# Position bias table in 128 partitions and a quarter of the query rows, and a later place for the RG-LRU constants and the modulation pieces

## The chip, the core and the metric

The kernel runs on one core of one Trainium2 chip. Its time is the device time of one execution in microseconds; lower is better. The times shown are the median of three runs. The trace comes from one profiled execution and counts from its first instruction.

## What is computed

A hybrid layer is followed by two modulated transformer layers, all for 256 tokens (and 256 context tokens) of 1024 features in float32. Only the hybrid layer bears on this change:

```
h    = rms_norm(x, norm_g[0]);  proj = h @ w_in      # split into the inputs of three mixers
y_a  = rglru_mixer(...)      # log_a = -8 * r * softplus(-lam): constants of lam, then a scan over tokens
y_b  = nsa_mixer(...)        # 16 heads; every score has + tbl[rel_bucket(t - s)][head]
y_c  = gla_mixer(...)        # gated linear attention in chunks of 32 tokens
x    = x + rms_norm((sum of gates * (y @ w_branch)) @ w_out, norm_g[1]);  x = x + rms_norm(swiglu(...))
```

The position bias of the second mixer depends on the distance between query and key alone: one row of 384 distances per head holds it. The two layers behind need modulation columns, `silu(c) @ ada_w + ada_b`, of which nothing depends on the hybrid layer.

## The kernel before, in words

**Dense products.** All weights come as tiles of 128 partitions x 1024 float32 (512 KB). `wload` (line 62) issues the load on SyncE's DMA queue (line 68), casts the tile to a high part `wh` on ScalarE (line 71), subtracts it to a low part `wl` on VectorE (line 72), and TensorE makes three products per block (lines 104, 105, 108; for the 512 column form lines 371 to 373). The pools `wraw`, `wh` and `wl` hold three tiles each, so SyncE can issue the load of a tile only when the low part of the tile three places ahead is done.

**Background work.** The modulation columns are made without TensorE. A piece (`Ada.chunk`, line 1052) loads 128 x 512 float32 (256 KB, `araw`, line 1056, three buffers) and runs two multiply-and-sum instructions on VectorE (line 1059, output `junk`). The first layer has 144 such pieces. `K.rate` says how many pieces are put into the program for each tile of weights that `wload` takes; `K.credit` carries the fraction. Here the rate is 0.35 through the whole hybrid layer, from a credit of -5.

**What sets the order.** The program text is not the order on the engines: the build places instructions on each engine's queue by what is ready, and text that stands earlier has the first claim. So a piece that stands late in the text still moves ahead into places that the build takes for free. Each engine then runs its own queue strictly in that order, and a waiting instruction holds all that stand behind it, SyncE's loads too.

**The bias table.** `nsa_bias` (line 340) makes T[head, distance] by one product of the 32 x 16 table `rel` with a one-hot matrix, adds the mask `neg` (line 351) and has 16 partitions with 384 numbers. It then writes each head's row 128 times to DRAM, one copy per query row of a tile, in four DMAs of 32 copies (line 354). `rel_bias` (line 523) reads two heads back as [128 queries, head, 256 distances] in one DMA whose row step is 383 instead of 384, which shifts each query row by one distance. It runs once for each of the 8 chunks of two heads.

**The order in the text** (`Block1.run`): norm, key and value chunks of the compressed branch, the RG-LRU constants (`lru_prep`, line 641), queries, `nsa_rows` (eight small DMAs `x<-kvc` that turn keys into rows), keys woven with `compress_units` and `gla_decay` (its running sums are the four scans of line 757), values, the queries of the gated attention, `nsa_bias`, its values (`gla_v_units`, 8 tiles) and keys (line 785), gates, `gla_steps` (first mask copy on line 827), and then a weave of RG-LRU, merge and branch products with the attention of the second mixer (line 576 adds the bias to the scores). Names: `lrut`, `lsp`, `lbh` are RG-LRU's constants, `gk`, `gq`, `gt`, `gb`, `gatt` belong to the gated attention, `x`, `kvc`, `blk` to the compressed branch, `cs` and `ccth` are the modulation's two input vectors.

Of the kernel before, what the change touches and what calls it, by code (L numbers as in the profile page):

```python
# [7 lines left out]
F32 = mybir.dt.float32  # L8
# [6 lines left out]
P = 128  # L15
# pieces of background work for each tile of weights, in the kernel's parts
RATE1, RATE2, RATE3, RATE4, RATE5 = 0.35, 0.8, 0.3, 1.1, 0.0
CALM, NG1, NG2, LEAD, TAIL, NPRE, WARM, D1, D2 = 16, 14, 24, 3, 5, 2, 13, 2, 3
# steps of small dependent work after each piece of dense products
# [5 lines left out]
class Core:  # L25
    def __init__(self, tc, ctx, D):
# [8 lines left out]
        # work to be traced along with the weight tiles, rate pieces for each  # L35
# [6 lines left out]
        # the tensor engine's clock rises while the first data come in  # L42
# [12 lines left out]
    def preload(self, *srcs, low=None):  # L55
        """the weight tiles that the next calls of wload want, ahead of other work; low: the engine for l"""
# [23 lines left out]
    def fill(self, n):  # L80
        """trace the next n pieces of background work"""
        for _ in range(min(n, len(self.filler))):
            self.filler.pop(0)()

    def calm(self, n):
        """no background work along with n weight tiles, while a chain counts"""
        self.credit -= n * self.rate
# [11 lines left out]
    def mm3(self, out, wts, acts, start=True, stop=True):  # L99
        """out (+)= sum_k w_k^T a_k; wts: [(h, l)] with [128, M], acts: [(h, l)] with [128, N]"""  # L100
# [9 lines left out]
    def rsqrt_small(self, x, n, scale, eps=1e-6):  # L110
        """1/sqrt(x*scale + eps) for x [128, n] (SBUF or PSUM); for more than a few columns by Newton's steps"""
# [22 lines left out]
    def gelu2_steps(self, out, x, tmp):  # L134
        """out = 2 * gelu(x) (tanh form) in two steps; x, tmp, out in SBUF"""
# [8 lines left out]
    def sq_acc(self, accs, src, m):  # L144
        """squares of chunk m of 8: summed in accs[0], the last one apart in accs[1]"""
# [8 lines left out]
    def accs(self):  # L154
        """two [128, 256] sums of squares for 256 tokens"""
        return [self.sp.tile([P, 256], F32, tag=f"acc{i}", name=self.nm(f"acc{i}")) for i in range(2)]

    def rstd(self, accs, n, d):
        """[128, n / 128]: 1/sqrt(sum_p sum(accs)[p, t] / d + eps), tokens on partitions"""
# [8 lines left out]
    def bcast_rows(self, r):  # L168
        """r [128, n] per token as [128, n * 128] PSUM, the same on every partition"""
# [10 lines left out]
    def norm_mod_into(self, zh, zl, X, rb, G, S, ms=range(8)):  # L180
        """chunks ms of z = X*rstd*G + S split into (h, l) [128, 8, 256]; G, S(m): columns (S None: no shift)"""
# [16 lines left out]
    def stagger(self, first, second, norm, ahead):  # L198
        """pieces of the two segments' last products; the norm that follows is begun for the first segment
# [1810 lines left out]
```

## Time and profile before

| what | before |
|---|---|
| device time, median of 3 runs | 2429.65 us (2429.4 to 2430.14) |
| span of the profiled execution (first to last instruction) | 2420.2 us |
| TensorE busy | 2358.1 us (97%) |
| VectorE busy | 1717.1 us (71%) |
| ScalarE busy | 1050.3 us (43%) |
| GpSimd busy | 184.6 us (8%) |
| read from and written to HBM | 389.38 MB and 8.13 MB |

The trace gives the span of the profiled execution and no other time of it; the median of the timed runs is 9.45 us longer than that span. The busy shares are means over stages with different limits. [...]

### The profile page before, as it was taken

How to read it: one execution, taken by the hardware profiler on the slowest of the kernel's cores; microseconds unless marked ns; L12 is line 12 of the kernel's file. 1: busy time of each engine (PE TensorE's matmuls, PEld its weight loads, DVE VectorE, ACT ScalarE, POOL GpSimd, SP SyncE). 2: the span in 40 equal slices, each digit the busy share in tenths (PEclk: the TensorE clock that was granted, in tenths of full speed). 3: DMA queues.
4: the chain of work that ended last, by engine and by line, in shares of the span. 5: the costliest groups of instructions: out<-in, count | busy, mean ns of one | idle time of the engine just before them, and what ended most of it. 6: DMA issues, size and time to landing. Idle time of an engine off the chain costs nothing.

```text
span 2420.2 us, 38663 instructions
## 1 busy us (share of the span) xinstructions
PE 2358.1 (97%) x14647; PEld 2070.7 (86%) x14647; DVE 1717.1 (71%) x3622; ACT 1050.3 (43%) x1879; POOL 184.6 (8%) x207
## 2 busy tenths in 40 slices
PE   9969999999999999999999999999999999998999
PEld 8858988899999998889768888888988888877999
DVE  7946798768899976438787865656865755856555
ACT  5522477456444532226764422223522223665443
POOL 1100021111000100012330000000100000101000
PEclk8989999999999999999999999999999999998999
DMA  7884533366788664465313644444653533533664
GB/s 238 252 196 154 172 110 123 109 197 191 255 264 251 203 214 137 131 191 162 124 60 127 213 157 135 152 135 147 209 165 123 165 126 114 181 109 106 191 183 157
DMA packets 159110, 401.10 MB, mean 166 GB/s; under 512 B 26763, under 2 KB 42427, under 8 KB 158923
## 3 DMA queue, kind: packets, MB, share of 16 engines
q1 hardware_dynamic: 158923, 398.62, 52.8%
q8 instruction: 115, 1.88, 0.3%
q14 instruction: 72, 0.59, 0.1%
HBM read 389.38 MB, written 8.13 MB: 164 GB/s over the span
## 4 chain that ended last, share of the span: by engine, by line
PE 83%; DVE 6%; issue 4%; DMA 3%; ACT 2%; POOL 1%; SPq 1%; DVEq 0%; ACTq 0%; POOLq 0%
PE ps_mm L104 23%; PE ps_mm L108 23%; PE ps_mm L105 23%; DVE wl L72 2%; PE ps_mm L1201 2%; PE ps_mm L1202 1%; PE ps_mm L1203 1%; PE ps_at L1318 1%; DMA wraw<-in_w_in_n 1%; DVE junk L1059 1%; PE ps_mm L574 1%; DMA araw<-in_ada_w 1%; PE ps_mm L1680 1%; ACT wh L71 1%; PE ps_mm L1450 1%
## 5 line engine op out<-in xcount | busy, mean ns | idle before, releaser
L71 ACT CAST wh<-wraw 128x1024 fp32r<-128x1024 f32 (+2 forms) x603 | 604.5, 1003 | 780.0 <-PE ps_mm L108 389.4
L72 DVE TENSOR_TENSOR wl<-wraw,wh 128x1024 fp32r<-128x1024 f32 (+2 forms) x601 | 706.9, 1177 | 317.3 <-ACT wh L71 309.4
L104 PE MATMUL ps_mm<-zh,wh 128*128 128x256 f32 (+1 forms) x2568 | 765.9, 323 | 5.4 <-ACT zh L190 2.8
L105 PE MATMUL ps_mm<-zh,wl 128*128 128x256 f32 (+1 forms) x2568 | 759.8, 321 | 2.3 <-DVE wl L72 2.3
L104 PEld LDWEIGHTS ps_mm<-zh,wh 128*128 128x128 f32 x2568 | 489.0, 191 | 61.7 <-issue 13.7
L105 PEld LDWEIGHTS ps_mm<-zh,wl 128*128 128x128 f32 x2568 | 489.3, 191 | 41.9 <-DVE wl L72 3.5
L108 PE MATMUL ps_mm<-zl,wh 128*128 128x256 f32 (+1 forms) x2568 | 455.7, 320 | 0.0
L108 PEld LDWEIGHTS ps_mm<-zl,wh 128*128 128x128 f32 x2568 | 380.5, 190 | 39.0 <-issue 1.3
L1059 DVE SCALAR_TENSOR_TENSOR junk<-araw,cs 128x512 f32<-128x512 f32 x576 | 391.1, 692 | 13.9 <-DMA araw<-in_ada_w 6.6
L104 PE MATMUL ps_mm<-hh,wh 128*128 128x256 f32 (+1 forms) x1021 | 313.6, 329 | 0.9 <-ACT wh L71 0.9
L105 PE MATMUL ps_mm<-hh,wl 128*128 128x256 f32 (+1 forms) x1021 | 311.5, 327 | 1.0 <-DVE wl L72 0.9
L104 PEld LDWEIGHTS ps_mm<-hh,wh 128*128 128x128 f32 x1021 | 192.8, 189 | 21.6 <-ACT wh L71 1.1
L105 PEld LDWEIGHTS ps_mm<-hh,wl 128*128 128x128 f32 x1021 | 193.0, 189 | 19.4 <-DVE wl L72 1.4
L108 PE MATMUL ps_mm<-hl,wh 128*128 128x256 f32 (+1 forms) x1021 | 194.0, 327 | 0.0
L263 ACT ACTIVATE silu<-ps_mm 128x256 f32<-128x256 f32 (+1 forms) x124 | 58.8, 474 | 302.5 <-PE ps_mm L108 290.3
L108 PEld LDWEIGHTS ps_mm<-hl,wh 128*128 128x128 f32 x1021 | 156.6, 189 | 18.5 <-DVE hl L266 0.4
L1148 DVE SCALAR_TENSOR_TENSOR X<-ps_mm,adac,X 128x256 f32<-128x256 f32 x128 | 61.7, 482 | 128.2 <-PE ps_mm L108 126.9
L264 DVE TENSOR_TENSOR silu<-silu,ps_mm 128x256 f32<-128x256 f32 (+1 forms) x124 | 65.8, 531 | 110.0 <-PE ps_mm L108 109.6
L116 POOL TENSOR_TENSOR rs_v<-rs_v,power 128x2 f32<-128x2 f32 (+1 forms) x17 | 24.1, 1420 | 1054.3 <-ACT wh L71 709.6
L1201 PE MATMUL ps_mm<-wh,zh 128*128 128x512 f32 (+1 forms) x224 | 87.0, 388 | 0.0
L1202 PE MATMUL ps_mm<-wh,zl 128*128 128x512 f32 (+1 forms) x224 | 85.4, 381 | 0.0
L1203 PE MATMUL ps_mm<-wl,zh 128*128 128x512 f32 (+1 forms) x224 | 85.3, 381 | 0.0
(378 smaller groups left out, 2619.1 us busy)
## 6 DMA issues: line engine op xcount, KB each, us to landing
wraw<-in_up SPq DMA_DIRECT2D x204, 512.0 KB, 3.6
araw<-in_ada_w SPq DMA_DIRECT2D x288, 256.0 KB, 3.4
wraw<-in_w_in_t SPq DMA_DIRECT2D x72, 512.0 KB, 3.7
wraw<-in_dn SPq DMA_DIRECT2D x79, 448.0 KB, 3.3
wraw<-in_f_up SPq DMA_DIRECT2D x44, 512.0 KB, 4.3
wraw<-in_dn SPq DMA_DIRECT2D x40, 512.0 KB, 3.8
wraw<-in_ev_in SPq DMA_DIRECT2D x26, 512.0 KB, 3.4
wraw<-in_w_br SPq DMA_DIRECT2D x24, 512.0 KB, 4.0
```

What stands on the lines that cost most here:

```text
L71: nc.scalar.copy(h[:, :cols], raw[:, :cols])
L72: (low or nc.vector).tensor_tensor(out=l[:, :cols], in0=raw[:, :cols], in1=h.bitcast(F32)[:, :cols], op=ALU.subtract)
L104: nc.tensor.matmul(out, wh, ah, start=start and k == 0, stop=False)
L105: nc.tensor.matmul(out, wl, ah, start=False, stop=False)
L108: nc.tensor.matmul(out, wh, al, start=False, stop=stop and k == n - 1)
L263: nc.scalar.activation(g, pair[0], AF.Silu)
L264: nc.vector.tensor_tensor(out=g, in0=g, in1=ps, op=ALU.mult)
L1059: nc.vector.scalar_tensor_tensor(out=junk, in0=raw, scalar=1.0, in1=self.cs[:, s, h * 512:(h + 1) * 512], op0=ALU.mult, op1=ALU.mult, accu ...
L1148: self.nc.vector.scalar_tensor_tensor(out=X[:, m, :], in0=ps, scalar=self.ada.c[l][:, j, m, s:s + 1], in1=X[:, m, :], op0=ALU.mult, op1=AL ...
L1201: nc.tensor.matmul(ps[i], z.zh[:, k, tk], wh[:, w], start=k == 0, stop=False)
L1202: nc.tensor.matmul(ps[i], z.zl[:, k, tk], wh[:, w], start=False, stop=False)
L1203: nc.tensor.matmul(ps[i], z.zh[:, k, tk], wl[:, w], start=False, stop=k == 7)
```

## The change

The bias product gets its table widened on GpSimd: every head stands on 8 partitions, so that 128 partitions hold 16 heads x 8 equal rows. One DMA writes each of them 4 times: 32 rows per head in place of 128, 768 KB in place of 3072 KB. The read back is done per 32 query rows, four DMAs for each chunk in place of one. `lru_prep` moves behind the keys of the gated attention in the text. The modulation pieces have rate 0 up to the values of the gated attention, 1.2 from there, 0 in the weave with the second mixer's attention, and 1.2 again in the last eight tiles; the credit starts at 0. The mask constant has 128 rows instead of 16. The comments are gone from the new file, so its line numbers differ by a few.

```diff
-RATE1, RATE2, RATE3, RATE4, RATE5 = 0.35, 0.8, 0.3, 1.1, 0.0
+RATE1, RATE_GLA, RATE2, RATE3, RATE4, RATE5 = 0.0, 1.2, 0.8, 0.3, 1.1, 0.0
...
-            neg = self.a4("neg", shape=(16, 384))
+            neg = self.a4("neg", shape=(P, 384))
             nc.sync.dma_start(neg, K.D["relneg"])
-            ps = K.psum("at")
-            nc.tensor.matmul(ps[:16, :384], rel, oh, start=True, stop=True)
-            nc.vector.tensor_tensor(out=neg, in0=neg, in1=ps[:16, :384], op=ALU.add)
-            self.rscr = self.tc.dram_tile([16, 128, 384], F32, name="rel_scratch")
-            for q in range(4):
-                nc.sync.dma_start(self.rscr[:, q * 32:(q + 1) * 32, :], neg[:, None, :].to_broadcast([16, 32, 384]))
+            wide = self.s1("t1", (P, 260))[:32, :P].rearrange("p (h c) -> p h c", c=8)
+            nc.gpsimd.tensor_copy(wide, rel[:, :, None].to_broadcast([32, 16, 8]))
+            ps = K.psum("at")[:, :384]
+            nc.tensor.matmul(ps, wide.rearrange("p h c -> p (h c)"), oh, start=True, stop=True)
+            nc.vector.tensor_tensor(out=neg, in0=neg, in1=ps, op=ALU.add)
+            self.rscr = self.tc.dram_tile([P, 4, 384], F32, name="rel_scratch")
+            nc.sync.dma_start(self.rscr[:, :, :], neg[:, None, :].to_broadcast([P, 4, 384]))
...
-            self.nc.sync.dma_start(B, bass.AP(tensor=base.tensor, offset=base.offset + (8 * a + r) * 128 * 384 + 127,
-                                              ap=[[383, 128], [4 * 128 * 384, 2], [1, 256]]))
+            for p in range(0, P, 32):
+                self.nc.sync.dma_start(B[p:p + 32], bass.AP(
+                    tensor=base.tensor, offset=base.offset + (8 * a + r) * 32 * 384 + 127 - p,
+                    ap=[[383, 32], [4 * 32 * 384, 2], [1, 256]]))
...
         self.small_proj()
-        self.lru_prep()
...
         self.gla_rest()
+        K.rate = RATE_GLA
         for f in self.gla_v_units(0) + self.gla_v_units(1) + units(self.gla_k, 4):
             f()
         og = units(self.gla_o, 8)
+        self.lru_prep()
...
+        K.rate = 0.0
         seq = b2[4:] + l0 + [then(l1[0], *a0)] + l1[1:] + [then(mg[0][0], *a1)] + mg[0][1:6]
...
+        K.rate = RATE_GLA
         for m in range(8):
             self.branch(1, lambda: self.pairs(self.ny), m, True)
...
-            K.filler, K.rate, K.credit = [ada.prep] + ada.pieces(0), RATE1, -5.0
+            K.filler, K.rate, K.credit = [ada.prep] + ada.pieces(0), RATE1, 0.0
```

Three places show how the queues move. First SyncE's queue where the bias table is written, before the change:

```order
L68 DMA wraw_1390<-in_w_in_n 128x1024
L1056 DMA araw_3417<-in_ada_w 128x512
L1056 DMA araw_3650<-in_ada_w 128x512
L68 DMA wraw_1412<-in_w_in_n 128x1024
L354 DMA rel_scratch<-neg_1313 16x32x384 x4
L68 DMA wraw_1436<-in_w_in_n 128x1024
L68 DMA wraw_1454<-in_w_in_n 128x1024
L68 DMA wraw_1472<-in_w_in_n 128x1024
L529 DMA relb_2688<-rel_scratch 128x2x256
L529 DMA relb_2690<-rel_scratch 128x2x256
L68 DMA wraw_1499<-in_w_in_t 128x1024
```

The same place on SyncE's queue after the change:

```order
L68 DMA wraw_1327<-in_w_in_n 128x1024
L68 DMA wraw_1355<-in_w_in_n 128x1024
L356 DMA rel_scratch<-neg_1225 512x1x384
L68 DMA wraw_1379<-in_w_in_n 128x1024
L68 DMA wraw_1409<-in_w_in_n 128x1024
L1063 DMA araw_2230<-in_ada_w 128x512
L68 DMA wraw_1433<-in_w_in_n 128x1024
L1063 DMA araw_2298<-in_ada_w 128x512
L68 DMA wraw_1460<-in_w_in_t 128x1024
L1063 DMA araw_2355<-in_ada_w 128x512
L68 DMA wraw_1499<-in_w_in_t 128x1024
```

One write stands in place of four, and three of the eight `w_in_n` loads of the gated attention's values stand behind it, as they did before; the read backs have gone further down and modulation loads stand between the weights.

Second, SyncE's queue near the start, at the eight loads that turn keys into rows, before the change:

```order
L68 DMA wraw_400<-in_w_in_t 128x1024
L1040 DMA ng_103<-in_ng 128x48
L393 DMA x_55_470<-kvc_211 64x2x256
L68 DMA wraw_432<-in_w_in_t 128x1024
L394 DMA x_55_470<-kvc_211 64x2x255
...
L68 DMA wraw_480<-in_w_in_t 128x1024
L393 DMA x_56_475<-kvc_211 64x2x256
L394 DMA x_56_475<-kvc_211 64x2x255
...
L68 DMA wraw_512<-in_w_in_t 128x1024
```

And after the change:

```order
L68 DMA wraw_362<-in_w_in_t 128x1024
L1050 DMA cs<-in_cc 128x1024
L68 DMA wraw_394<-in_w_in_t 128x1024
L395 DMA x_55_432<-kvc_211 64x2x256
L396 DMA x_55_432<-kvc_211 64x2x255
...
L395 DMA x_56_437<-kvc_211 64x2x256
L396 DMA x_56_437<-kvc_211 64x2x255
...
L68 DMA wraw_442<-in_w_in_t 128x1024
L68 DMA wraw_474<-in_w_in_t 128x1024
```

The eighth weight tile (`wraw_480` before, `wraw_442` now) stood ahead of the second group of key rows (`x_56`) and now stands behind it, and the load of `cs` has come up to the sixth tile.

Third, VectorE's queue behind the sum of the bias table, before the change, with the low parts of the first tiles of the gated attention's values:

```order
L351 TENSOR_TENSOR neg_1313<-neg_1313,ps_at_1315 16x384
L776 TENSOR_TENSOR gt_740<-gb_741 128x1024
...
L72 TENSOR_TENSOR wl_1415<-wraw_1412,wh_1414 128x1024
L1069 TENSOR_TENSOR adac_106<-adac_106,ada_b 128x16
L72 TENSOR_TENSOR wl_1439<-wraw_1436,wh_1438 128x1024
L72 TENSOR_TENSOR wl_1457<-wraw_1454,wh_1456 128x1024
L72 TENSOR_TENSOR wl_1475<-wraw_1472,wh_1474 128x1024
L72 TENSOR_TENSOR wl_1502<-wraw_1499,wh_1501 128x1024
```

And after the change:

```order
L354 TENSOR_TENSOR neg_1225<-neg_1225,ps_at_1229 128x384
L780 TENSOR_TENSOR gt_702<-gb_703 128x1024
...
L72 TENSOR_TENSOR wl_1358<-wraw_1355,wh_1357 128x1024
L1066 SCALAR_TENSOR_TENSOR junk_2176,adapart<-araw_2174,cs 128x512
L1066 SCALAR_TENSOR_TENSOR junk_2178,adapart<-araw_2174,cs 128x512
L72 TENSOR_TENSOR wl_1382<-wraw_1379,wh_1381 128x1024
L1066 SCALAR_TENSOR_TENSOR junk_2232,adapart<-araw_2230,cs 128x512
L1066 SCALAR_TENSOR_TENSOR junk_2234,adapart<-araw_2230,cs 128x512
L1075 TENSOR_TENSOR adac_106<-adapart 128x16
L1076 TENSOR_TENSOR adac_106<-adac_106,ada_b 128x16
L72 TENSOR_TENSOR wl_1412<-wraw_1409,wh_1411 128x1024
```

Where the low parts of four tiles stood in a row, each now has two modulation instructions beside it. Counted over the whole queue from this sum to the first `gatt` copy, both orders hold 14 low parts; the modulation instructions are 19 before and 30 now. From the low part of the sixth tile to the scans of line 757 they are 20 before and 22 now, with 17 of the RG-LRU constants' instructions added, which stood ahead of the sixth tile. From the scans to the sum of the table the modulation instructions are 20 in both, with 11 of RG-LRU's added. At the 65th weight tile SyncE's queue has issued 51 modulation loads before and 54 now; at the 145th it is 53 and 54, and from the 155th on the two agree within two loads to the end.

## Rows read from the trace of the kernel before

**Rows 1.** The page's chain that ended last, by engine.

```profile
PE 83%; DVE 6%; issue 4%; DMA 3%; ACT 2%; POOL 1%; SPq 1%; DVEq 0%; ACTq 0%; POOLq 0%
```

**Rows 2.** Stretches: busy us (x instructions) per engine, clock, DMA share, GB/s.

```profile
28.57:76.84 48.27, 48.07 (x378) 45.65 (x378) 44.00 (x87) 31.64 (x46) 0.00 (x0) 1.00 0.89 289
76.84:116.15 39.31, 35.18 (x214) 30.36 (x213) 34.98 (x72) 19.22 (x25) 6.76 (x6) 0.91 0.77 244
129.96:153.07 23.11, 0.00 (x0) 0.00 (x0) 0.02 (x1) 1.04 (x1) 0.00 (x0) 0.61 0.93 151
153.07:185.02 31.95, 31.41 (x200) 28.11 (x200) 25.53 (x52) 14.40 (x18) 0.00 (x0) 0.91 0.82 265
288.20:476.80 188.60, 186.43 (x1346) 163.25 (x1346) 164.28 (x458) 119.95 (x303) 33.60 (x53) 1.00 0.37 118
```

**Rows 3.** TensorE in order of time: start, us, form, idle before and its end.

```profile
129.34 0.39 PE L372 MATMUL ps_mm<-wh,zl 128*128 128x512 f32 x1
129.57 0.39 PE L373 MATMUL ps_mm<-wl,zh 128*128 128x512 f32 x1
153.07 0.80 PE L371 MATMUL ps_mm<-wh,zh 128*128 128x512 f32 x1 [23.12 <-ACT wh L71]
...
158.75 0.40 PE L371 MATMUL ps_mm<-wh,zh 128*128 128x512 f32 x1
```

**Rows 4.** SyncE's queue in order of time, around the bias table's write.

```profile
116.72 13.21 SPq L354 DMA_DIRECT2D rel_scratch<-neg  x4
130.03 13.16 SPq L68 DMA_DIRECT2D wraw<-in_w_in_n  x3
150.53 0.89 SPq L529 DMA_DIRECT2D relb<-rel_scratch  x2
```

**Rows 5.** One stretch while the table is written, columns as in rows 2.

```profile
118.00:148.00 30.00, 11.96 (x53) 9.57 (x51) 5.86 (x12) 4.21 (x5) 0.00 (x0) 0.78 0.92 103
```

**Rows 6.** The table's DMAs: issue duration ns min/median/max, first and last start us.

```profile
L529 SPq DMA_DIRECT2D relb<-rel_scratch x8: 377/377/464, 150.5 to 429.9; - x8
L354 SPq DMA_DIRECT2D rel_scratch<-neg x4: 345/4040/4642, 116.7 to 125.6; - x4
```

**Rows 7.** DMA issues: count, KB each, median us from issue to landing.

```profile
wraw<-in_w_in_n SPq DMA_DIRECT2D x12, 512.0 KB, 3.5
...
rpb<-rpb_scratch SPq DMA_DIRECT2D x32, 64.0 KB, 3.1
```

**Rows 8.** VectorE in order of time, in the keys of the gated attention.

```profile
164.94 0.69 DVE L1059 SCALAR_TENSOR_TENSOR junk<-araw,cs 128x512 f32<-128x512 f32 x1
...
165.55 1.22 DVE L72 TENSOR_TENSOR wl<-wraw,wh 128x1024 fp32r<-128x1024 f32 x1
166.69 0.68 DVE L1059 SCALAR_TENSOR_TENSOR junk<-araw,cs 128x512 f32<-128x512 f32 x1
...
167.31 0.42 DVE L785 TENSOR_TENSOR gk<-ps_mm,gz 128x256 f32<-128x256 f32 x1
167.65 0.41 DVE L786 TENSOR_TENSOR gb<-ps_mm,gt 128x256 f32<-128x256 f32 x1
```

**Rows 9.** VectorE at the RG-LRU constants.

```profile
28.21 0.17 DVE L661 TENSOR_TENSOR lrut<-lrut 128x8 f32<-128x8 f32 x1
```

**Rows 10.** SyncE's queue, then ScalarE, at the eighth weight tile.

```profile
27.90 0.56 SPq L68 DMA_DIRECT2D wraw<-in_w_in_t  x1
30.08 0.60 SPq L393 DMA_DIRECT2D x<-kvc  x1
...
33.24 1.05 ACT L71 CAST wh<-wraw 128x1024 fp32r<-128x1024 f32 x1 [0.45 <-DMA wraw<-in_w_in_t]
...
41.51 0.38 ACT L418 ACTIVATE qT<-ps_mm 128x256 f32<-128x256 f32 x1 [0.55 <-PE ps_mm L108]
```

**Rows 11.** Windows in which the granted clock fell, columns as in rows 2.

```profile
80.00:90.00 10.00, 7.76 (x28) 6.39 (x29) 9.01 (x19) 5.32 (x8) 1.50 (x1) 0.68 0.58 183
...
200.00:210.00 10.00, 10.00 (x56) 9.25 (x55) 4.94 (x10) 2.29 (x4) 0.00 (x0) 0.68 0.25 80
```

More of the change, by code (lines that the diff above doesn't have):

```diff
@@ L1877, in _shape_constants @@
     C["onehot"] = oh
-    neg = np.zeros((16, 384), np.float32)
+    neg = np.zeros((128, 384), np.float32)
     neg[:, 256:] = -1e30
```

## The prediction

> **What bounds the kernel now.** I began with the chain of waits: 83% of it is TensorE [rows 1], so a change can gain only where TensorE stands still or runs at its lower clock. I then looked at the span in short stretches for such places in the hybrid layer, since from the 155th weight tile on the order of loads is the same within two. There is one large place: from 129.96 to 153.07 us TensorE does nothing, and neither do the other engines, while the DMA engines are 93% busy [rows 2]. TensorE's own rows show the end of it: the idle time of 23.12 us ended with a cast, which had waited for a weight tile [rows 3]. SyncE's queue shows why the tile was late: the four writes of the bias table occupy its issue for 13.21 us, the next three weight loads go out from 130.03 us on, and the read back, which waits for the last write, at 150.53 us [rows 4]. The first write was issued in 345 ns, the later ones took some 4 us each [rows 6], so the queue was full. The writes are what fills it: 4 x 786,432 B = 3.15 MB at 103 GB/s [rows 5] is 30.5 us, from 116.72 to about 147 us, with the DMA engines 92% busy all the time. Weights move at 289 GB/s at a share of 0.89 [rows 2].
>
> The stall has a tail. Before it, matmuls of 512 columns start 0.23 us apart. The 12 from 153.07 to 158.75 us take 5.68 us instead of 12 x 0.23 = 2.76 us [rows 3], 2.92 us more, and the mean clock of the idle stretch is 0.61 [rows 2]. The stall and its tail are 23.12 + 2.92 = 26.0 us.
>
> **The change part by part.**
>
> *The write.* It carries a quarter, 786,432 B. At the weights' 289 GB/s that is 2.7 us, at the rate of the old write, 103 GB/s, 7.6 us. What must hide it: when the table was ready, five of the eight tiles of values were loaded or loading, which kept TensorE at work from 116.7 to 129.96 us, 13.3 us. The sixth tile has to land and be split in that time: 3.5 us [rows 7] and then 1.05 us for the cast [rows 10] and 1.22 us for the low part [rows 8], 5.8 us. With the write ahead of it that is 8.5 to 13.4 us: hidden at the one end, 0.1 us late at the other. I take 0; without the cover it would cost its 2.7 to 7.6 us. Then the stall and its tail go: **-26.0 us**.
>
> Which end is nearer depends on why the old write was slow, and no row tells that apart from a slow DRAM side, as every long stretch at 103 GB/s is this one write from 16 partitions. [...]
>
> *The wide table* is one GpSimd copy (that engine is busy 8% of the span) ahead of a product that has the same 384 columns, and the larger mask is 168 KB more to load early, 0.6 us of DMA at 289 GB/s; the sum on VectorE has the same 384 elements per partition. Nothing of it is waited for longer: 0.
>
> *The read back* is four issues of 64 KB for one of 256 KB. One issue now holds SyncE 377 ns [rows 6], four 1.5 us, 1.1 us more for each of eight chunks. In the weave TensorE works 186.43 of 188.60 us [rows 2], with a weight tile each 2.9 us or more (24 products of 256 columns, each half of the 0.23 us of 512) on three buffers, and so 1.1 us more in the queue is hidden. I take 0, with 8 x 1.1 = 9 us as the price if no buffer covered it.
>
> *RG-LRU's constants and the modulation pieces, first stretch.* From the sixth tile's low part (28.57 us) to the scans (76.84 us) VectorE gets 2 more modulation instructions and 17 of RG-LRU's. Price from the rows: a modulation instruction takes a place of 0.61 us (164.94 to 165.55) [rows 8], one of RG-LRU's 0.17 us [rows 9]: 1.2 + 2.9 = 4.1 us. VectorE is busy 44.00 of 48.27 us there, so 4.3 us are free [rows 2]. All of it may fit, or all may be late, since the engine runs strictly in order; the DMA engines are at 0.89 here too. Bounds 0 to 4.1 us, nearer the low end as the free time is just enough: **+1.5**. From there to the sum (76.84 to 116.15 us) 11 of RG-LRU's at 0.17 us, 1.9 us, meet 4.3 us free: 0.
>
> *The eighth weight tile.* Its load went out at 27.90 us and now stands behind the second group of key rows, whose first goes out at 30.08 us as soon as ScalarE has the last chunk; four issues at 0.60 us put it to about 32.5 us, 4.6 us later [rows 10]. The cast at 33.24 us had waited for this tile [rows 10]. With 1.05 us for it and 1.22 us for the low part the tile was ready by about 35.5 us, and TensorE took it for the product that ends at 41.51 us, so from about 41.5 - 2.9 = 38.6 us. Of 4.6 us, 3.1 are covered: 0 to 1.5 us, I take the middle, **+0.8**.
>
> *Values and keys of the gated attention.* From the sum (116.15 us) to the first mask copy (185.02 us) VectorE gets 11 more modulation instructions, 30 for 19: 11 x 0.61 = 6.7 us. Its whole work there becomes 14 x 1.14 (low parts, 165.55 to 166.69) + 30 x 0.61 + 8 x 0.34 (key products, 167.31 to 167.65) [rows 8] + some 2.5 for the rest = 39.5 us. TensorE's time for the stretch, without the stall and its tail, is 68.9 - 26.0 = 42.9 us. It fits with 3.4 us to spare, by a margin of 8%. The DMA engines are as close: 14 tiles, 15 pieces, the write, two read backs and RG-LRU's weights are 13.1 MB, at 289 GB/s 45 us, at a share of 1 (289/0.89 = 325) 40 us. Bounds 0 to 6.7 us; nearer the low end, since it fits in both sums: **+2.0**. Behind it, up to the weave, the same 11 instructions are gone, where TensorE hardly waits: 0.
>
> *The later parts.* In the weave no modulation piece stood before and none stands now, so the rate 0 there changes nothing; behind it the loads agree within two. 0.
>
> **Sum.** -26.0 + 1.5 + 0.8 + 2.0 = -21.7 us. Against the profiled span that is 2420.2 - 21.7 = 2398.5 us; the runs are 9.45 us longer than this span, so the median comes to 2429.65 - 21.7 = **2408.0 us**.
>
> **The rivals.**
>
> *More is given back.* If VectorE's order costs all of its bounds, 4.1 + 1.5 + 6.7 = 12.3 us come back: 2429.65 - 26.0 + 12.3 = 2416.0 us, and with one more fall of the clock of the kind in rows 11 (68% over 10 us, so 3.2 us lost) 2419. For it: VectorE was busy 91% of the first stretch already. Against it: the counts fit.
>
> *More is gained.* Two windows at a clock of 0.68 [rows 11] cost 3.2 us each, and TensorE idles 4.1 us between the scans and the sum [rows 2]. Three low parts instead of two now stand ahead of the scans. If one fall and half of the idle time go and nothing else comes, the time is 2403.6 - 3.2 - 2.0 = 2398 us.
>
> *It does not do what it says.* If SyncE's issue stays blocked, because 512 rows of 1.5 KB occupy it as before whatever their source, or the table comes later than now, the stall is only moved: 2425 to 2430 us. Against it: the first of the four writes left SyncE after 345 ns [rows 6].
>
> *Slower.* The read back holds SyncE's queue in the weave. If the four parts landed one after another, each in the 3.1 us of a 64 KB read back of a similar table [rows 7], and SyncE could not go on before, 12.4 us per chunk would meet two tiles' cover of 5.8 us: 6.6 us for each of 7 chunks, 46 us, and 2408 + 46 = 2454 us. It decides from 26.5/7 = 3.8 us per chunk on. Against it: SyncE waits for buffers, not for landings, and one read back held it 377 ns.
>
> **How the numbers follow.** The forecast (2403 to 2412 us) has 0.65, more given back (2412 to 2420) 0.16, more gained (2396 to 2403) 0.11, not doing what it says 0.05, slower 0.03. From 2398 to 2418 us holds four fifths and reaches into both neighbours. Runs of this kernel tell 0.2%, 4.9 us, from no change: faster by more 0.92, within it 0.05 (most of the third rival), slower 0.03.
>
> **What the changed profile would show.** The write: one issue under 1 us, no stretch of 10 us without TensorE between 110 and 170 us, no long stretch of DMA at 100 GB/s. The given back: TensorE waits on a low part around 38 us, before the scans, and in the gated attention's keys, each under 4 us, with VectorE over 95% busy there. The weave as long as now, near 188 us. I am wrong if TensorE still waits over 8 us for a `w_in_n` tile, if the waits on low parts sum to over 10 us, or if the weave grows.

## The result and the profile after

| | before | after |
|---|---|---|
| median of the timed runs | 2429.89 us (2429.4 to 2431.06, 4 runs) | 2396.89 us (2394.53 to 2397.43, 4 runs) |
| ratio, 95% interval | | 0.9872 (0.9852 to 0.9892) |
| span of the profiled execution, clock | 2420.2 us, 0.985 | 2395.7 us, 0.990 |
| TensorE busy | 2358.1 us | 2356.5 us |
| written to HBM | 8.13 MB | 5.77 MB |

The kernel is faster by 33.0 us in the medians and by 24.5 us between the two profiled executions. The forecast was 21.7 us and 2408.0 us: the direction is right, the time is 11.1 us below the forecast and 1.1 us below the low end of its range.

The chain that ended last on the page after, by engine. TensorE's share has risen from 83% to 88%, and "issue" has fallen from 4% to 1% [rows 1]:

```profile
PE 88%; DVE 5%; DMA 2%; ACT 2%; POOL 2%; issue 1%; SPq 0%; ACTq 0%; DVEq 0%; POOLq 0%
```

Stretches of the kernel after, columns as in rows 2: around the write, the weave, and one window to which I come back.

```profile
110.00:170.00 60.00, 60.00 (x380) 53.33 (x380) 54.64 (x124) 24.20 (x29) 0.31 (x1) 0.98 0.87 281
262.93:451.50 188.57, 186.49 (x1346) 163.31 (x1345) 164.43 (x458) 119.89 (x303) 33.40 (x53) 1.00 0.39 118
40.00:50.00 10.00, 9.37 (x44) 8.26 (x45) 6.77 (x13) 5.54 (x11) 0.00 (x0) 0.66 0.69 225
```

TensorE is busy in all of the 60 us from 110 to 170, where it stood still for 23 us before, and the DMA engines move 281 GB/s there; while the old table was written they moved 103 GB/s [rows 5]. The weave has the length and the busy time that it had [rows 2]. SyncE's queue around the write of the kernel after: one issue of 0.58 us where four took 13.21 [rows 4], and the next weight loads go out 2.3 us after it.

```profile
118.16 2.02 SPq L68 DMA_DIRECT2D wraw<-in_w_in_n  x2
121.40 0.58 SPq L356 DMA_DIRECT2D rel_scratch<-neg  x1
123.67 2.69 SPq L68 DMA_DIRECT2D wraw<-in_w_in_n  x2
```

The read backs (the view of line 532: duration in ns, minimum, median, maximum) are 32 for 8 [rows 6]; under "who waited for it" that view names no engine.

```profile
L532 SPq DMA_DIRECT2D relb<-rel_scratch x32: 325/420/669, 141.4 to 406.3; - x32
```

To compare stages I use three marks on TensorE: the first product with `zh`, the table's product and the first transpose of `gb` in the gated attention. They are these rows of before,

```profile
115.30 0.81 PE L350 MATMUL ps_at<-oh,rel 32*16 32x384 f32 x2
178.63 0.60 PE L795 MATMUL ps_at<-ident,gb 128*128 128x128 f32 x4
```

and these of after:

```profile
13.79 0.58 PE L104 MATMUL ps_mm<-zh,wh 128*128 128x256 f32 x1 [1.01 <-ACT zh L190]
...
119.87 0.58 PE L353 MATMUL ps_at<-oh,t 32*128 32x384 f32 x1
...
157.03 0.60 PE L799 MATMUL ps_at<-ident,gb 128*128 128x128 f32 x4
```

From the table's product to `gb` it was 178.63 - 115.30 = 63.33 us and is 157.03 - 119.87 = 37.16 us: -26.2 us. From the first product (13.41 us before) to the table's product it was 101.89 us and is 106.08 us: +4.2 us. The first product itself starts 0.4 us later, and what is behind `gb` takes 2.9 us less: 26.2 - 4.2 - 0.4 + 2.9 = 24.5 us.

### The profile page after: what moved, and what is told of

The parts are those of the page before. It is cut to its first block, busy times and chain, and to the rows that moved or that the text cites. A ratio compares the mean times of both kernels' runs of the same rounds, so it can differ in the third digit from the quotient of the medians.

```text
span 2395.7 us, 38691 instructions
## 1 busy us (share of the span) xinstructions
PE 2356.5 (98%) x14647; PEld 2072.7 (87%) x14647; DVE 1715.2 (72%) x3622; ACT 1049.3 (44%) x1879; POOL 183.7 (8%) x208
## 3 DMA queue, kind: packets, MB, share of 16 engines
HBM read 389.56 MB, written 5.77 MB: 165 GB/s over the span
## 4 chain that ended last, share of the span: by engine, by line
PE 88%; DVE 5%; DMA 2%; ACT 2%; POOL 2%; issue 1%; SPq 0%; ACTq 0%; DVEq 0%; POOLq 0%
PE ps_mm L104 24%; PE ps_mm L105 24%; PE ps_mm L108 24%; PE ps_mm L1208 2%; PE ps_mm L1210 2%; PE ps_mm L1209 2%; DVE wl L72 1%; PE ps_at L1325 1%; PE ps_mm L1457 1%; PE ps_mm L578 1%; PE ps_at L1314 1%; ACT wh L71 1%; DMA wraw<-in_up 1%; DVE junk L1066 1%; PE ps_mm L1687 1%
## 5 line engine op out<-in xcount | busy, mean ns | idle before, releaser
L1066 DVE SCALAR_TENSOR_TENSOR junk<-araw,cs 128x512 f32<-128x512 f32 x576 | 391.0, 693 | 11.1 <-DMA araw<-in_ada_w 3.7
```

The costliest lines, as they stand in the source:

```text
L1066: nc.vector.scalar_tensor_tensor(out=junk, in0=raw, scalar=1.0, in1=self.cs[:, s, h * 512:(h + 1) * 512], op0=ALU.mult, op1=ALU.mult, accu ...
```

## The experiments

**Two parts of a run's time.** Every timed run has a span and a mean granted clock, as a share of TensorE's full clock. Span x clock is the time at full clock that the run's stretches are worth; span x (1 - clock), the rest, is what the lower clock took, and where TensorE stands still at the lower clock it counts a part of that idle time too. The clock is on record with three decimals, so both parts are uncertain by 1.2 us in a single run. The table has the mean of these two over the runs of each kernel, and its two stages (first product to table's product, table's product to `gb`) from its profiled execution, for the second row from the first profile of before. Device times are 1.7 to 1.9 us above the spans throughout.

| kernel | runs | median us | ratio (95%) | span x clock | rest | to the table | to `gb` |
|---|---|---|---|---|---|---|---|
| before, as its own run | 10 | 2426.34 | 1.0005 (0.9989 to 1.0021) | 2384.9 | 40.5 | 100.1 | 63.4 |
| before, beside the others | 46 | 2425.0 to 2428.9 | 1 | 2385.0 to 2385.4 | 38.5 to 41.9 | 101.9 | 63.3 |
| after, first | 4 | 2396.89 | 0.9872 (0.9852 to 0.9892) | 2370.7 | 23.9 | 106.1 | 37.2 |
| after, again | 5 | 2397.96 | 0.9874 (0.9849 to 0.9898) | 2369.8 | 27.3 | 103.1 | 37.2 |
| table alone | 4 | 2404.13 | 0.9912 (0.9887 to 0.9938) | 2370.4 | 31.2 | 100.1 | 37.2 |
| moves alone | 9 | 2429.4 | 1.0027 (1.0007 to 1.0046) | 2386.9 | 42.4 | 100.1 | 63.9 |
| table and constants | 6 | 2397.22 | 0.9878 (0.9857 to 0.99) | 2369.7 | 27.6 | 101.3 | 37.2 |
| table and rates | 4 | 2408.18 | 0.9914 (0.9888 to 0.994) | 2372.5 | 34.3 | 102.6 | 37.2 |
| eighth tile first | 10 | 2403.75 | 0.9933 (0.9905 to 0.9961) | 2369.6 | 37.1 | 101.3 | 37.2 |
| all rows, 128 partitions | 4 | 2407.96 | 0.9919 (0.9892 to 0.9946) | 2377.4 | 30.7 | 103.2 | 39.3 |
| quarter, 16 partitions | 6 | 2411.59 | 0.993 (0.9904 to 0.9956) | 2373.8 | 36.6 | 103.5 | 37.2 |
| after, 1.9 us later | 6 | 2409.84 | 0.9925 (0.9904 to 0.9945) | 2372.8 | 35.7 | 103.2 | 37.1 |
| after, 3.8 us later | 6 | 2413.67 | 0.9931 (0.9915 to 0.9947) | 2377.2 | 33.4 | 109.5 | 37.1 |

The delays of the last two rows are part of their column "to the table". The intervals of the table alone, table and rates, and all rows touch those of after, so that they differ from it is not beyond doubt; the intervals of the eighth tile first, the quarter and the two delays lie clear of it.

No kernel here leaves out any part of what has to be computed.

**The kernel before, once more.** No edit.

> The kernel before, unchanged, run once more as a run of its own, to see how its timed runs stand to its profiled execution. Its first profile had a span of 2420.2 us while its timed runs have a median of 2429.9 us; the changed kernel's runs are 1.7 us above their spans. If the timed runs of the kernel before have spans of about 2428 us, the 8 us lie inside the program and its profiled execution was a quick one; if their spans are about 2420 us and the times 2430 us, they lie around the program. The profile should show the idle time of TensorE of 23 us at about 130 us again.

Its ten runs have spans of 2420.4 to 2430.5 us and times of 2422.14 to 2432.34 us, 1.7 to 1.9 us above them. So the 8 us lie inside the program, and the profiled execution that I read was a quick one. Span x clock is 2383 to 2387 us in all ten; the rest, the time at the lower clock, goes from 34 to 46 us. In its profile TensorE stands still for 23.22 us at the write.

**The two halves of the change.** The table alone is after without the moves (first diff), the moves alone are after without the table's part (second):

```diff
-RATE1, RATE_GLA, RATE2, RATE3, RATE4, RATE5 = 0.0, 1.2, 0.8, 0.3, 1.1, 0.0
+RATE1, RATE2, RATE3, RATE4, RATE5 = 0.35, 0.8, 0.3, 1.1, 0.0
...
         self.small_proj()
+        self.lru_prep()
...
-            K.filler, K.rate, K.credit = [ada.prep] + ada.pieces(0), RATE1, 0.0
+            K.filler, K.rate, K.credit = [ada.prep] + ada.pieces(0), RATE1, -5.0
...
```

```diff
-            self.rscr = self.tc.dram_tile([P, 4, 384], F32, name="rel_scratch")
+            self.rscr = self.tc.dram_tile([16, 128, 384], F32, name="rel_scratch")
+            for q in range(4):
+                nc.sync.dma_start(self.rscr[:, q * 32:(q + 1) * 32, :], neg[:, None, :].to_broadcast([16, 32, 384]))
...
```

> The table's part of the change alone: 128 partitions, a quarter of the query rows, read back in four DMAs; RG-LRU's constants, the rates and the credit stay as before. Theory (the write's stall is the whole gain, and the moves cost some 4 to 6 us ahead of the sum and give some 4 us back behind it): the stall of 23.1 us and its tail of 2.9 us go, the table's product stands at 115.3 us as before, and the span is 2420.2 - 26.0 = 2394 us, within 3 us of the changed kernel's 2395.7; the eighth tile of values and keys costs no wait at 40 us. Rival 1 (the moves are part of the gain): without them the span stays above 2400 us, a ratio to before over 0.991. Rival 2 (the moves cost on balance): the span is 2390 us or less, faster than the changed kernel.

> The other part of the change alone: RG-LRU's constants, the modulation pieces' rates and the credit as in the changed kernel; the table is written for all 128 query rows from 16 partitions and read back in one DMA per chunk, as before. Theory: the stall at the write stays, 23 us of idle TensorE before a w_in_n tile, beginning some 5 us later than before because of the wait for the eighth tile near 40 us; the span is 2418 to 2426 us, ratio 0.998 to 1.002. Rival 1 (the moves are part of the gain): 2410 us or less, ratio below 0.996. Rival 2 (the moves cost): over 2424 us.

The moves alone keep the stall: TensorE's row of that kernel behind it is

```profile
153.62 0.80 PE L372 MATMUL ps_mm<-wh,zh 128*128 128x512 f32 x1 [23.62 <-ACT wh L71]
```

and its profiled span of 2422.8 us is that of the kernel before. The stall begins at 130.0 us as before, not 5 us later as I had expected, since no wait for the eighth tile came in this profile. Its ratio, 1.0027, lies just above what the theory allowed, and the mean span of its nine runs, 2429.3 us, is that of the rival by which the moves cost (over 2424 us); before has 2423.9 us beside it. Of the 5.4 us between them 1.5 are time at full clock and 3.9 the rest. The table alone has the same 37.16 us behind the table's product as the whole change, and a span x clock of 2370.4 us beside 2370.2 (the mean of the nine runs of after). So the table brings all of the gain at full clock, and the moves neither gain nor cost there by more than a microsecond or two. Its profiled span was 2396.1 us, as the theory had it (within 3 us of 2395.7). But its four runs spread from 2397.88 to 2407.58 us, with a mean span of 2401.6 us and a ratio of 0.9912, which is by the letter the rival that the moves are part of the gain. If they are, it is through the clock, and with these few runs that stays open.

**The missing combinations of the moves.** With the table's change go the rates alone (first diff against after: the constants are back) or RG-LRU's constants alone (second: rates and credit are back):

```diff
         self.small_proj()
+        self.lru_prep()
...
         og = units(self.gla_o, 8)
-        self.lru_prep()
```

```diff
-RATE1, RATE_GLA, RATE2, RATE3, RATE4, RATE5 = 0.0, 1.2, 0.8, 0.3, 1.1, 0.0
+RATE1, RATE2, RATE3, RATE4, RATE5 = 0.35, 0.8, 0.3, 1.1, 0.0
...
```

> The changed kernel with RG-LRU's constants back at their old place, so that the eighth tile is loaded between the two groups of key rows again; the table and the rates stay changed. If the wait for the eighth tile belongs to the moved constants, there is no wait near 40 us here, the table's product stands 100 to 102 us behind the first product, and the kernel is 3 to 6 us faster than the changed one of the same call. Rival (the constants' place does nothing that lasts): within 2 us of the changed kernel of the same call, apart from the spread of the granted clock.

> The table's change and RG-LRU's constants moved, with the modulation pieces' rates and credit as before: the piece that is missing between the table alone (2403 us at 0.987 on average, clock times span 2370) and the whole change (2398 us, 2370). Theory (the moved constants delay the eighth tile and nothing else, and the rest is the clock): TensorE waits near 40 us for 0.5 to 2 us, the first product to the table's product takes 102 to 106 us, clock times span is 2370 to 2374 us, and the median 2398 to 2410 us goes with the clock. Rival (the rates make the wait near 40 us): no wait there, 100 to 101 us to the table's product.

In neither does TensorE wait near 40 us. With the rates alone the table's product stands 102.6 us behind the first one, yet the kernel is not faster than after but 10 us slower in the median, at a rest of 34.3 us: the expectation that it would gain 3 to 6 us failed. With the constants alone the build leaves the eighth tile between the two groups of key rows, as before, so the theory for that run failed too: the late load comes only from both moves together, as the rates alone don't bring it either. Its rows on SyncE's queue:

```profile
26.92 0.55 SPq L68 DMA_DIRECT2D wraw<-in_w_in_t  x1
28.77 0.59 SPq L395 DMA_DIRECT2D x<-kvc  x1
```

**What made the old write slow: its source or its bytes.** Two kernels undo one of them each, all rows from 128 partitions and read back in one DMA per chunk (first), and a quarter of the rows from 16 partitions (second, where the product and the mask go back to 16 rows as well). Of each diff the write:

```diff
-            self.rscr = self.tc.dram_tile([P, 4, 384], F32, name="rel_scratch")
-            nc.sync.dma_start(self.rscr[:, :, :], neg[:, None, :].to_broadcast([P, 4, 384]))
+            self.rscr = self.tc.dram_tile([P, 16, 384], F32, name="rel_scratch")
+            nc.sync.dma_start(self.rscr[:, :, :], neg[:, None, :].to_broadcast([P, 16, 384]))
...
```

```diff
-            self.rscr = self.tc.dram_tile([P, 4, 384], F32, name="rel_scratch")
+            self.rscr = self.tc.dram_tile([16, 32, 384], F32, name="rel_scratch")
+            nc.sync.dma_start(self.rscr[:, :, :], neg[:, None, :].to_broadcast([16, 32, 384]))
...
```

> The changed kernel with the table written for all 128 query rows (16 copies from each of 128 partitions, 3.15 MB in one DMA) and read back in one DMA per chunk as before: only the source's partitions are changed, not the bytes. Theory 1 (the source of 16 partitions made the old write slow): it runs at 250 to 310 GB/s, takes 10 to 13 us, and TensorE stands still for 0 to 6 us at about 135 us; ratio to before 0.987 to 0.992. Theory 2 (the rows written in DRAM, 2,048 of 1.5 KB, make it slow): it runs at about 103 GB/s for 30 us, TensorE stands still for 20 to 24 us, and the time is that of the kernel before, ratio 0.997 to 1.002.

> The changed kernel with the quarter of the rows written from 16 partitions (32 copies of each, 786 KB in one DMA), read back in four DMAs: only the bytes are changed, not the source. Theory 1 (the source of 16 partitions is slow): it runs at about 103 GB/s for 7.6 us, and the weight tiles behind it land that much later; the cover of 13 us hides it but for 0 to 2 us of idle TensorE near 133 us, so the ratio to before is that of the changed kernel, or up to 0.001 above. Theory 2 (the bytes and rows make it slow): it runs as fast as the write from 128 partitions, at 250 GB/s or more, with no stretch of 5 us at about 100 GB/s. Either way the bytes alone would bring most of the 26 us.

With all rows from 128 partitions, the stretch behind the write's issue (columns as in rows 2), and TensorE's wait behind it:

```profile
122.46:131.00 8.54, 8.54 (x39) 7.07 (x38) 6.26 (x16) 2.89 (x4) 0.00 (x0) 1.00 1.03 367
```

```profile
134.91 0.50 PE L373 MATMUL ps_mm<-wh,zh 128*128 128x512 f32 x1 [1.47 <-ACT wh L71]
```

The DMA engines move 367 GB/s there, and TensorE loses 39.29 - 37.16 = 2.1 us in place of 26. The trace holds the write's 2,048 packets of 1,536 B: from the first to the end of the last they take 8.96 us, so 3.15 MB at 351 GB/s, where the same packets of the old write take 32.3 us. With a quarter of the rows from 16 partitions, one stretch, and VectorE's first low part behind it:

```profile
124.00:126.00 2.00, 2.00 (x10) 1.66 (x9) 1.85 (x5) 1.05 (x1) 0.00 (x0) 1.00 0.91 99
```

```profile
132.28 1.23 DVE L72 TENSOR_TENSOR wl<-wraw,wh 128x1024 fp32r<-128x1024 f32 x1 [3.49 <-ACT wh L71]
```

The rate is 99 GB/s, as slow as the old write's 103, at a DMA share of 0.91; the 512 packets take 7.6 us, and those of after 2.97 us. One packet takes 228 ns in the old write and 224 ns in this one, 65 ns in the two writes from 128 partitions (medians). So it is the source that makes the write slow, not the rows or the bytes. What changes along with its 16 partitions is how often one DMA repeats a source row: 32 times in both slow writes, 16 and 4 times in the fast ones. No run here separates the two. The stage to `gb` is 37.2 us all the same, so TensorE is covered. But VectorE stands idle for 3.5 us there. In the gated attention TensorE then waits 2.44 us for a mask copy, which stood behind a modulation instruction that had waited 1.31 us for its load. That this goes back to the slow write is not shown: with the table alone, too, TensorE waits 1.3 us for this copy.

So either half of the table's change takes nearly the whole stall away: the bytes alone 26.2 us of it, the source alone 24.1 us. The medians of the source alone and the bytes alone are 10 and 14 us above after; of that 7.2 and 3.6 us are time at full clock, the other part is the clock. Of the 7.2 us the stage to `gb` holds 2.1; where the others lie was not followed.

**The late eighth tile.** The load that RG-LRU's constants and the rates had pushed back is asked for first:

```diff
+        K.preload(K.D["w_in_t"][2])
         self.nsa_rows()
```

> The changed kernel with one load moved: the eighth of the first tiles of input weights is asked for ahead of the key rows' DMAs instead of behind them, which is where RG-LRU's constants had put it. Theory (the wait of 2.0 us near 40 us and the lower clock behind it, 0.66 in the window from 40 to 50 us, come from this late load): the wait is gone, the clock in that window is 0.9 or more, and the table's product stands 3 to 6 us earlier than the 119.9 us of the changed kernel; the span is 2391 to 2395 us. Rival (the lower clock or the wait comes from VectorE's order, with the modulation pieces and constants): TensorE waits as long at another place ahead of 60 us, and the span stays within 1.5 us of 2395.7 us.

> The changed kernel, unchanged, run and profiled once more beside the other runs of this call. In its first profile TensorE waited 2.0 us for the eighth tile at 40.6 us and ran at half clock behind it (6 us late at the table's product against the kernel before); with the moves alone (the profile of the run with the old table) the same order of loads cost no wait at all. Theory A (the wait is a close finish between the key rows' landing, VectorE's copies and the cast, and differs from one execution to the next): the wait at about 40 us is under 1 us here and the table's product stands 100 to 102 us behind the first product, for 106.1 in the first profile. Theory B (it belongs to the order): the wait is 1.5 to 2.5 us again and the product stands 104 to 107 us behind the first. Timed: a ratio of 0.985 to 0.992 to the kernel before.

These are rows of the first profile of after: SyncE, ScalarE and TensorE at the eighth tile.

```profile
33.01 1.72 SPq L68 DMA_DIRECT2D wraw<-in_w_in_t  x3
```

```profile
38.59 1.04 ACT L462 CAST blkh<-blk 128x1024 fp32r<-128x1024 f32 x1 [1.44 <-DVE blk L459]
39.54 1.04 ACT L71 CAST wh<-wraw 128x1024 fp32r<-128x1024 f32 x1
```

```profile
40.63 0.38 PE L104 MATMUL ps_mm<-zh,wh 128*128 128x256 f32 x1 [2.00 <-ACT wh L71]
```

The load goes out at 33.01 us, 5.1 us later than before [rows 10], but that is not what the tile waits for in the end. Its cast stands in ScalarE's queue behind the cast of `blkh`, which waits 1.44 us for VectorE's `blk`, and follows it without a wait of its own. VectorE had in turn waited for the key rows to land before its first copy of the group, 1.37 us in this profile, 0.67 us in the second one of after, and not at all in that of the shorter delay, where TensorE does not wait either. TensorE waits 2.00 us, and behind that the granted clock in 40 to 50 us is 0.66, 0.34 x 10 = 3.4 us lost. In the second profile of after the wait is

```profile
39.03 0.38 PE L104 MATMUL ps_mm<-zh,wh 128*128 128x256 f32 x1 [0.64 <-ACT wh L71]
```

and the clock there 0.83. The seven profiles with this order of loads have waits of 2.00, 0.64, 0.97, 1.57, 0, 1.85 and 0 us (after twice, all rows, quarter, the two delays, moves alone): a close finish, as theory A had it, which cost a wait in five of seven. The first stage is 100.1 us with the moves alone, where it does not come, and 106.1 and 103.1 us in after; the last lies between the two theories.

With the eighth tile first the wait for its cast is gone; TensorE waits 0.79 us for a low part at 44.26 us, and the clock in 40 to 50 us is 1.00. The table's product stands 101.3 us behind the first product, 4.8 and 1.8 us sooner than in the two profiles of after. Yet the median is 2403.75 us, 6 us above after, at the same span x clock (2369.6), with a rest of 37.1 us for 25.8. Neither the theory's span (2391 to 2395 us) nor the rival's is what was measured (2401.4).

**Small shifts.** The source of the last two kernels adds nothing but a delay: products of 128 columns ahead of the table's product, 8 or 16 of them (the diff has the first).

```diff
+            for _ in range(8):
+                nc.tensor.matmul(ps[:, :P], K.ones, K.ones, start=True, stop=True)
             nc.tensor.matmul(ps, wide.rearrange("p h c -> p (h c)"), oh, start=True, stop=True)
```

> The changed kernel with 8 more products of 128 columns on TensorE (their result is not used) just ahead of the table's product: 16 instructions at about 0.12 us each, a delay of 1.9 us, and nothing else changed. It asks why kernels whose time at full clock is alike (mean clock times span 2368 to 2376 us for all with a quarter of the rows) differ by 6 to 14 us in the median. Theory (small shifts decide which of the marginal falls of the granted clock come, in the gated attention and near 530, 780, 1230 and 1310 us): clock times span is 2372 us, 1.9 us above the changed kernel's 2370, but the median is 2403 to 2412 us, at a clock of 0.984 to 0.988. Rival (the falls belong to waits that the other versions have and this one doesn't): the median is 2398 to 2402 us at 0.988 to 0.990.

> The same with 16 more products, a delay of 3.8 us ahead of the table's product. Theory (small shifts decide): clock times span 2374 us, and the clock goes its own way again, 0.983 to 0.990, not in step with the delay of half the size. Rival (the falls belong to waits of the other versions): 2400 to 2404 us, 3.8 us above the changed kernel at the same clock.

The expectation had nothing else changed, but that is not so. The build, which places instructions by what is ready, gives the loads and VectorE's instructions another order in places. On SyncE's queue three weight loads stand in a row right ahead of the write with the shorter delay, two in after, and behind it two are left of the eight `w_in_n` loads, for three in after:

```profile
115.28 4.35 SPq L68 DMA_DIRECT2D wraw<-in_w_in_n  x3
```

With 1.9 us and that order the median is 12 us longer, with 3.8 us 16 us longer. Span x clock grows by 2.6 and 7.0 us, the rest by 10 and 8 us. The 7.0 us are more than the 3.8 expected; the wait of 1.85 us for the eighth tile is among them in its profile. The same 20 us of the gated attention, first in after, then with the delay of 1.9 us:

```profile
225.00:245.00 20.00, 19.94 (x158) 18.61 (x157) 13.93 (x24) 7.89 (x12) 1.64 (x1) 1.00 0.39 118
```

```profile
225.00:245.00 20.00, 20.00 (x87) 18.41 (x87) 5.17 (x11) 3.23 (x5) 1.65 (x1) 0.50 0.24 74
```

TensorE is busy the whole time in both, and with the delay also for all of the 35 us ahead; at a granted clock of 0.50, where after has 1.00, it gets through 87 products instead of 158. So the kernels with a quarter of the rows differ from each other by the clock, and a change as small as this one, a shift of 2 us and what it moves on the queues, is enough to change it. Shift and order are not separated. The rival, that falls belong to waits which only the other versions have, fails with this kernel: in the gated attention TensorE waits no more than 0.2 us. With table and rates and in the quarter a wait of 1.4 and 2.4 us for the mask copy does stand where the clock falls (161 and 163 us), so there it may have a part.

## Why the prediction was right, and where it was off

**The stall and its tail, -26.0 us: right.** The stage from the table's product to `gb` is 26.2 us shorter in every kernel with the quarter table. In span x clock the stall was worth 23.11 x 0.61 = 14.1 us and in the rest 23.11 x 0.39 + 2.92 = 11.9 us [rows 2, 3].

**The write hidden, 0: right, at the fast end.** The write's packets take 2.97 us, for 2.7 and 7.6 us at the two ends. The source decides, as the kernel with all rows shows (351 GB/s by its packets) and the one with 16 partitions (99 GB/s). I had left open why the old write was slow; it is the source's doing. At the slow end TensorE would have been covered too (37.2 us), but VectorE would not (3.49 us idle).

**The wide table and the read back, 0: right.** The read back's issue is 0.42 us for a quarter in place of 0.38 for the whole, and the weave took 188.57 us for 188.60.

**The first stretch, +1.5, and the eighth tile, +0.8: the waits came, but the stage grew by more, for a reason that I had not counted.** The first stage is 106.1 and 103.1 us against 101.9 and 100.1 before, +3.6 us on average for 2.3. These are the stretches of after up to the scans and from there to the table's product, columns as in rows 2:

```profile
28.60:81.40 52.80, 48.93 (x355) 46.40 (x354) 46.49 (x107) 30.43 (x46) 0.00 (x0) 0.91 0.83 260
81.40:119.87 38.47, 36.48 (x231) 31.93 (x231) 35.07 (x80) 19.73 (x26) 6.22 (x7) 0.94 0.81 262
```

Up to the scans TensorE stands still for 3.87 us here and 2.73 us in the second profile of after, 0.20 and 0.37 us in those of before: 3.0 us more on average. Of the 3.87 and 2.73 us, 2.00 and 0.64 are the eighth tile; the first is above my bounds of 0 to 1.5. Of the others 0.6 and 1.0 us are waits on VectorE's low parts, for which the 1.5 us stood, and 1.3 and 1.1 us waits on ScalarE's casts. From the scans to the table's product it stands still for 1.99 and 2.49 us in place of 4.13 and 3.27, 1.5 us less on average, where I had 0.

That the eighth tile's wait lies near what I took is luck: I followed its load, and the wait came from the casts of `blkh` ahead of it on ScalarE. The second thing that I left out is the lower clock behind that wait, 3.4 us in one execution and 1.7 us (0.17 x 10) in the other. A slip in the price: RG-LRU's instructions stand 0.20 us apart in the trace of before, not 0.17, so the upper bound was 4.6 us and not 4.1.

**Values and keys of the gated attention, +2.0: wrong, it is 0.** The stage of 37.16 us is the same with 11 more modulation instructions (after) and without (table alone), and it is what 63.33 - 26.0 = 37.3 us leaves. VectorE was busy 54.64 of 60 us from 110 to 170 us; the work fitted. Of my two sums only VectorE's said so plainly; the one for the DMA engines gave 45 us at 289 GB/s against 42.9, and 40 only at a share of 1. They moved 301 GB/s at a share of 0.91 in this stage. I priced the narrow margin, and nothing of it came. The rival by which more is given back falls with it.

**The later parts, 0: not exactly.** Behind `gb` the two profiles of after are 2.9 and 2.5 us shorter than those of before. Falls of the clock come and go there from run to run (500 to 700 us: 1.00 and 0.97 in the two profiles of before, 0.99 and 1.00 in those of after), so this is not one place.

**The base, 2429.65 us: too high by 2.5 us.** I took 9.45 us between span and median as something around the program. It lies inside: runs are 1.8 us above their own spans, the three runs that I had were long ones, and the profiled execution was quick. The 56 runs of before in these tables have a mean span of 2425.3 us, a time of 2427.1.

**The sum.** Means over all runs: span x clock fell from 2385.2 to 2370.2 us, -15.0, of which the stall is 14.1; the rest fell from 40.0 to 25.8 us, -14.2, of which the stall and its tail are 11.9. So beside the 26.0 us, 0.9 and 2.3 us more went, where I had 4.3 us coming back. 2429.65 - 2.5 - 26.0 - 0.9 - 2.3 = 2398.0 us, for medians of 2396.89 and 2397.96. That is the time of the rival "more is gained" (2398 us, 0.11), but only in part its way: the rest fell by 2.3 us, a little less than its one fall of the clock; of the 2.0 us of idle time that it took, 1.5 went between the scans and the table's product, but 3.0 came ahead of the scans. In the four profiles alone the change is -25.1 us on average (2420.85 to 2395.8): 3.6 of the 4.3 us of costs came, in the first stage, and 2.7 us went behind `gb`. The other runs of before were longer by their rest, which makes the other 4.1 us, and in which stage is not seen. So the mechanism of the main term is right, the sum of the small ones was not: their size hangs on the clock, for which the forecast had no term but the stall's tail. The rival "it does not do what it says" fails on the write's 0.58 us, the slower one on the weave.

**What stays open.** Versions with equal span x clock, 2370 us within 1, have medians from 2397 to 2404 us, and one with 2372.8 us, the shorter delay, has 2410 us. That the clock makes the difference is shown; what in a version decides how many falls come is not. Executions of one kernel differ, 2391.32 to 2410.89 us for table and constants, and the means of versions differ as well, 2398.9 against 2410.4 us (after again, five runs; with the shorter delay, six). The delay also moved instructions on the queues, so which of the two makes that difference is not shown. No version here beats after: table and constants equals it.

## What to carry to other kernels

A small transfer that is broadcast from few partitions can cost nearly as much as a large one: 0.79 MB from 16 partitions took 7.6 us here, 3.15 MB from 128 took 9.0 us. Read the GB/s of the stretch beside the DMA share (103 at 0.92 here), and when many loads stand behind such a write in one queue, spread its source over all partitions or cut its bytes; here either one took nearly the whole stall away. Before a profiled span is used as the base of a sum, see how the timed runs scatter around it, and split each run into span x clock and the rest; an edit whose effect shows in one of the two alone is read from that one. A load that is moved must be followed through the engine queue that consumes it, not only to its landing: the cast here stood behind another cast that was late.

## What the runs showed of the hardware that I had not expected

- A granted clock of 0.50 stood for 20 us while TensorE was busy for all of the 20 us (the row at 225 to 245 us with the delay). In these rows neither busy time nor waits tell when it will fall.
- The clock spreads the ten runs of the kernel before over 10 us, at a span x clock of 2383 to 2387 us, which is not much more than its rounding.
- One DMA from 128 partitions had 3.15 MB and the loads behind it at 367 GB/s, above the 289 GB/s at which I had priced weights [rows 2].
- A packet of 1,536 B took 228 and 224 ns in the two writes from 16 partitions and 65 ns in the two from 128 (medians).
